# Scores of a pair of chunks as three products of 64 stationary columns on alternating halves of the output

## The chip, the cores and the metric

The kernel runs on one core of a Trainium2 chip. The metric is the device time of one execution in microseconds (us). TensorE multiplies matrices and writes to PSUM, VectorE (DVE) and ScalarE (ACT) work elementwise, GpSimd (POOL) helps them, and SyncE (SP) starts most transfers between HBM and SBUF. Each engine has its own instruction stream and works through it in the order in which the instructions stand; semaphores connect the streams.

## The reference

A block of a streaming encoder on one sequence of 2048 tokens of width 1024. A normalised input is projected (1024 to 2560 columns); one half of the mixer is a gated linear recurrence (HGRN2) of 4 heads of 128 in chunks of 64 tokens, the other a diagonal state-space layer (S5). Their outputs are projected, and a gated MLP with a short convolution follows. What the change touches is the recurrence within a chunk:

```python
b = jnp.cumsum(logf, axis=3)
q_dec = qh * jnp.exp(b)
k_dec = k * jnp.exp(-b)
mask = jnp.tril(jnp.ones((CHUNK, CHUNK), dtype=bool))
att = jnp.einsum('bhnck,bhnsk->bhncs', q_dec, k_dec)
att = jnp.where(mask, att, 0.0)
o_intra = jnp.einsum('bhncs,bhnsv->bhncv', att, vh)
```

A state carries what earlier chunks leave to later ones.

## The kernel before, in words

The program has three stages: projections with recurrence and S5 (its last scores start at 628 us), the output projection (its matmuls from 676 to 892 us), and the MLP. The first stage runs over 80 slots, 40 for each half of the sequence. In a slot `project` (L231 to L233) makes 128 columns of the projection for 512 tokens, 24 matmuls of 128 stationary and 512 moving columns, and hands them to the S5 part or to a unit of the recurrence. A `Unit` is one head and 512 tokens; there are 16 (4 heads, 2 halves, 2 blocks of 512).

A unit joins its 8 chunks of 64 tokens to 4 pairs. It keeps `kt`, for each pair three blocks of 64 key columns: block 0 is the first chunk's keys, block 2 the second's, block 1 the first's keys scaled by the first chunk's whole decay, so that queries of the second chunk can be held against them. `qb` has the queries in the same way; blocks 0 and 2 are the ones read here. `keys` (L628 to L633) and `query` make them on VectorE and ScalarE. `scores` multiplies them into one PSUM tile `pa` of 128 partitions (keys) by 4 pairs of 128 columns (queries): first-chunk keys with first-chunk queries fill partitions 0 to 63 of columns 0 to 63 (L648), and blocks 1 and 2 together, 128 stationary columns, with second-chunk queries fill all partitions of columns 64 to 127 (L649). Keys and queries are float32. VectorE then masks `pa` into `attm`, which a later slot multiplies with the values (`outputs`, L712); `flip_keys` (L667) transposes the scaled keys for the states.

The S5 part has products that the prediction draws on: `scan` (L500) makes 8 matmuls of 64 stationary and 128 moving columns that write partitions 0 to 63 and 64 to 127 by turns; `kernel_rows` (L562 to L565) has small matmuls of 32 stationary columns; `output_map` (L587, L588) has full ones. All are float32.

What order the instructions stand in is set by a scheduler at build time. It takes them as the slots issue them, and places each on its engine by its own estimate of durations, so a change of some instructions can move others by a few places.

Of the kernel before, what the change touches and what calls it, by code (L numbers as in the profile page):

```python
# [41 lines left out]
def _bc(ap, dim, n):  # L42

    a = ap.unsqueeze(dim)
    shape = list(a.shape)
    shape[dim] = n
    return a.to_broadcast(shape)


def _body(ctx, tc, A, out, dbg=None):  # L50
    nc = tc.nc
    VE, SC, GP, PE = nc.vector, nc.scalar, nc.gpsimd, nc.tensor
    dma = nc.sync.dma_start

    def tt(eng, o, a, b, op):
        eng.tensor_tensor(o, a, b, op=op)  # L56
# [91 lines left out]
    with ExitStack() as p1:  # L148
# [451 lines left out]
        class Unit:  # L600
# [43 lines left out]
            def scores(self):  # L644
                pa = ps_od.tile([P, 4, P], F32, tag="od", name="ps_att")
                kt, qb = self.kt, self.qb
                for i in range(4):
                    PE.matmul(pa[0:64, i, 0:64], kt[:, i, 0], qb[:, i, 0], start=True, stop=True)  # L648
                    PE.matmul(pa[:, i, 64:128], kt[:, i, 1:3].rearrange("p b t -> p (b t)"), qb[:, i, 2],  # L649
                              start=True, stop=True)  # L650
                am = attms[self.tb]
                tt(VE, am[0:64, :, 0:64].bitcast(I32), pa[0:64, :, 0:64].bitcast(I32),
                   _bc(mask[0:64, 0:64], 1, 4), ALU.bitwise_and)
                tt(VE, am[:, :, 64:128].bitcast(I32), pa[:, :, 64:128].bitcast(I32),
                   _bc(mask[:, 64:128], 1, 4), ALU.bitwise_and)
                self.ks = hp.tile([P, 4, P], F32, tag="ks", name="ks")
                for i in range(4):
                    SC.activation(self.ks[:, i], kt[:, i, 1:3].rearrange("p b t -> p (b t)"), AF.Copy, scale=self.e2[:, i])
# [100 lines left out]
        for hf in range(2):  # L759
# [12 lines left out]
            for bt in range(8):  # L772
                s0 = 40 * hf + 10 + (27 * bt + 6) // 8
                b = S5(hf, bt)
# [33 lines left out]
        for hf in range(2):  # L808
            for n in range(40):
# [31 lines left out]
                if cb < 4:  # L841
                    if cb % 2 == 0:
                        ut = sp.tile([P, 2, TS, 64], F32, tag="wt", name="ut", bufs=2)
                    t = ut[:, cb % 2]
# [252 lines left out]
    with ExitStack() as p3:  # L1097
        pa = p3.enter_context(ExitStack())
# [530 lines left out]
```

## Time and profile before

| | us |
|---|---|
| median of 3 runs | 2310.33 |
| lowest, highest | 2306.52, 2311.77 |
| profiled execution | 2313.69 |
| its span, first to last instruction | 2311.9 |
| TensorE busy in the span | 2207.9 |
| VectorE busy | 1712.9 |
| ScalarE busy | 990.7 |

The profile's rows name a line of the kernel, an engine, an operation and its tiles as out<-in. PE is TensorE's matmuls, PEld its loads of stationary columns. In a timeline row the first number is the start, the second the time to the end of the last of the instructions that the row merges, xN their count. Ends of matmuls are modelled, so a matmul lasts longer in a row than it holds the array; what counts for pace is the step from start to start. Matmuls in float32 leave two records each; those of the projections, in a rounded float32, leave one.

### The profile page before, as it was taken

How to read it: one execution, taken by the hardware profiler on the slowest of the kernel's cores; microseconds unless marked ns; L12 is line 12 of the kernel's file. 1: busy time of each engine (PE TensorE's matmuls, PEld its weight loads, DVE VectorE, ACT ScalarE, POOL GpSimd, SP SyncE). 2: the span in 40 equal slices, each digit the busy share in tenths (PEclk: the TensorE clock that was granted, in tenths of full speed). 3: DMA queues.
4: the chain of work that ended last, by engine and by line, in shares of the span. 5: the costliest groups of instructions: out<-in, count | busy, mean ns of one | idle time of the engine just before them, and what ended most of it. 6: DMA issues, size and time to landing. Idle time of an engine off the chain costs nothing.

```text
span 2311.9 us, 28187 instructions
## 1 busy us (share of the span) xinstructions
PE 2207.9 (96%) x10120; PEld 1771.8 (77%) x10120; DVE 1712.9 (74%) x2615; ACT 990.7 (43%) x1770; POOL 765.6 (33%) x696
## 2 busy tenths in 40 slices
PE   8999999999989998899999988999999899999996
PEld 6778778888868876688888866888888677777775
DVE  9887786666664325887777778777777688788787
ACT  5333353232254334555555564555555423233343
POOL 1111100000000004555555555655555234445432
PEclk9899999999999999899999988999999999999998
DMA  6465655334434333222222222222222622222223
GB/s 226 143 210 178 188 183 162 124 125 131 141 87 136 116 119 109 83 97 83 83 80 82 78 91 82 93 82 82 83 82 73 227 83 84 71 90 75 68 88 119
DMA packets 143790, 262.18 MB, mean 113 GB/s; under 512 B 43936, under 2 KB 67360, under 8 KB 143648
## 3 DMA queue, kind: packets, MB, share of 16 engines
q1 hardware_dynamic: 138896, 243.05, 32.4%
q0 software_dynamic: 4752, 17.30, 2.0%
q8 instruction: 80, 1.31, 0.2%
q14 instruction: 62, 0.51, 0.1%
HBM read 178.52 MB, written 81.79 MB: 113 GB/s over the span
## 4 chain that ended last, share of the span: by engine, by line
PE 72%; DVE 16%; issue 5%; DMA 3%; ACT 2%; POOL 1%; SPq 0%; DVEq 0%; POOLq 0%; ACTq 0%
PE ps_u L1168 19%; PE ps_v L1168 9%; PE ps_out L975 6%; PE ps_du L1361 6%; PE ps_pj L231 5%; PE ps_pj L233 5%; PE ps_pj L232 5%; PE ps_w L1168 5%; PE ps_dv L1361 3%; DVE accp L62 2%; DVE gvl L65 2%; PE ps_dn L1448 1%; DMA graw<-gv_d 1%; DVE cv L65 1%; PE ps_att L649 1%
## 5 line engine op out<-in xcount | busy, mean ns | idle before, releaser
L231 PE MATMUL ps_pj<-xh,wh 128*128 128x512 f32 x640 | 261.9, 409 | 6.6 <-ACT xh L201 6.4
L232 PE MATMUL ps_pj<-xl,wh 128*128 128x512 f32 x640 | 256.4, 401 | 0.0
L233 PE MATMUL ps_pj<-xh,wl 128*128 128x512 f32 x640 | 256.0, 400 | 0.0
L74 DVE SCALAR_TENSOR_TENSOR cv<-cv,par 128x1024 f32<-128x1024 f32 x176 | 237.1, 1364 | 25.3 <-ACT cv L1180 23.4
L132 ACT ACTIVATE uh<-us 128x512 fp32r<-128x512 f32 x176 | 110.5, 630 | 195.6 <-PE ps_u L1168 93.4
L56 POOL TENSOR_TENSOR us<-uraw 128x512 f32<-128x512 f32 x88 | 121.8, 1384 | 215.4 <-DMA uraw<-in_wup_dram 149.7
L65 DVE TENSOR_TENSOR ul<-us,uh 128x512 fp32r<-128x512 f32 x132 | 156.2, 1184 | 1.6 <-ACT uh L132 1.5
L1361 PE MATMUL ps_du<-dh,gvh 128*128 128x512 f32 x320 | 131.9, 412 | 25.3 <-DVE accp L62 16.8
L132 ACT ACTIVATE uh<-uraw 128x512 fp32r<-128x512 f32 x132 | 83.5, 632 | 159.0 <-PE ps_u L1168 81.0
L231 PEld LDWEIGHTS ps_pj<-xh,wh 128*128 128x128 f32 x640 | 121.9, 190 | 37.2 <-ACT xh L201 6.4
L233 PEld LDWEIGHTS ps_pj<-xh,wl 128*128 128x128 f32 x640 | 121.6, 190 | 29.5 <-issue 1.1
L232 PEld LDWEIGHTS ps_pj<-xl,wh 128*128 128x128 f32 x640 | 121.7, 190 | 28.2 <-issue 1.5
L1361 PE MATMUL ps_du<-dl,gvh 128*128 128x512 f32 x320 | 128.6, 402 | 0.0
L1361 PE MATMUL ps_du<-dh,gvl 128*128 128x512 f32 x320 | 128.6, 402 | 0.0
L65 POOL TENSOR_TENSOR ul<-us,uh 128x512 fp32r<-128x512 f32 x44 | 68.6, 1560 | 173.0 <-ACT uh L132 170.6
L132 ACT ACTIVATE gvh<-gs 128x512 fp32r<-128x512 f32 x80 | 50.4, 630 | 162.3 <-POOL gs L56 81.6
L62 DVE TENSOR_TENSOR accp<-accp,ps_du 128x1024 f32<-128x1024 f32 (+1 forms) x84 | 97.7, 1163 | 28.7 <-PE ps_du L1361 28.3
L1180 ACT ACTIVATE cv<-cv,par 128x1024 f32<-128x1024 f32 x88 | 109.7, 1246 | 19.3 <-DVE cv L62 17.9
L56 POOL TENSOR_TENSOR gs<-graw 128x512 f32<-128x512 f32 x38 | 58.6, 1542 | 160.8 <-DMA graw<-gv_d 135.0
L1361 PEld LDWEIGHTS ps_du<-dh,gvh 128*128 128x128 f32 x320 | 61.7, 193 | 48.9 <-issue 23.8
L975 PE MATMUL ps_out<-wo,ogp 128*128 128x512 f32 x384 | 95.5, 404 | 0.9 <-DVE og L74 0.9
L515 POOL MEMSET z<- 128x4 f32 x16 | 1.7, 104 | 284.7 <-DVE zi L65 212.7
(438 smaller groups left out, 6237.4 us busy)
## 6 DMA issues: line engine op xcount, KB each, us to landing
uraw<-in_wup_dram SPq DMA_DIRECT2D x86, 512.0 KB, 3.5
gv_d<-cv SPq DMA_DIRECT2D x43, 512.0 KB, 2.6
graw<-gv_d SPq DMA_DIRECT2D x84, 256.0 KB, 3.3
wraw<-in_win_dram SPq DMA_DIRECT2D x24, 512.0 KB, 4.5
xt<-in_wdown_dram SPq DMA_DIRECT2D x44, 256.0 KB, 3.0
ws_d<-wh POOLq DMA_DIRECT2D x16, 512.0 KB, 3.5
ws_d<-wl POOLq DMA_DIRECT2D x16, 512.0 KB, 6.0
wh<-ws_d SPq DMA_DIRECT2D x16, 512.0 KB, 4.0
```

Source lines behind the costliest of these rows:

```text
L56: eng.tensor_tensor(o, a, b, op=op)
L62: eng.tensor_tensor(o, a, b, op=ALU.add)
L65: eng.tensor_tensor(o, a, b, op=ALU.subtract)
L74: eng.scalar_tensor_tensor(o, a, s, b, op0=op0, op1=op1)
L132: SC.activation(h, raw, AF.Copy)
L231: PE.matmul(ps, a, xh, start=(kt == 0), stop=False)
L232: PE.matmul(ps, a, xl, start=False, stop=False)
L233: PE.matmul(ps, b, xh, start=False, stop=(kt == KT - 1))
L975: PE.matmul(pss[nh], parts[lp][kt][:, tq], wo[rp][kt][:, nh * BLK : (nh + 1) * BLK], start=first, stop=last)
L1168: PE.matmul(ps, l, r[kt], start=(fresh and first), stop=end, skip_group_check=not fresh)
L1180: SC.activation(c, cin[:, 2 : HALF + 2], AF.Identity, scale=tap[2], bias=par[:, C_CB + cb : C_CB + cb + 1])
L1361: PE.matmul(ps[:, i], l[:, j, i * P : (i + 1) * P], r, start=(fresh and n == 0), stop=(n == 5), skip_group_check=not fresh)
```

## The change

The two products of a pair become three. All have 64 stationary and 64 moving columns. The product of 128 stationary columns is cut into its halves: block 2 with the second chunk's queries goes to partitions 64 to 127, block 1 with the same queries to partitions 0 to 63. The first product stays. In the order of issue a pair writes partitions 0 to 63, 64 to 127, 0 to 63. A unit has 12 matmuls instead of 8, and TensorE 64 more in all.

```diff
                 for i in range(4):
-                    PE.matmul(pa[0:64, i, 0:64], kt[:, i, 0], qb[:, i, 0], start=True, stop=True)
-                    PE.matmul(pa[:, i, 64:128], kt[:, i, 1:3].rearrange("p b t -> p (b t)"), qb[:, i, 2],
-                              start=True, stop=True)
+                    for rows, cols, k, q in ((0, 0, 0, 0), (64, 64, 2, 2), (0, 64, 1, 2)):
+                        PE.matmul(pa[rows : rows + 64, i, cols : cols + 64], kt[:, i, k], qb[:, i, q],
+                                  start=True, stop=True)
```

In the scheduled order fifteen of the sixteen units now stand as twelve matmuls in a row on TensorE. The fifth unit (237 us in the trace of before) is the other one. There products of the S5 output map, `ps_y`, stand between the scores `ps_att`:

```order
-L648 MATMUL ps_att<-qb,kt 64x64
+L649 MATMUL ps_att<-qb,kt 64x64 x2
 L587 MATMUL ps_y<-ug,mt 128x128
-L649 MATMUL ps_att<-qb,kt 128x64
-L648 MATMUL ps_att<-qb,kt 64x64
+L649 MATMUL ps_att<-qb,kt 64x64 x10
 L588 MATMUL ps_y<-xs,tv 128x128
-L649 MATMUL ps_att<-qb,kt 128x64
-L648 MATMUL ps_att<-qb,kt 64x64
-L649 MATMUL ps_att<-qb,kt 128x64
-L648 MATMUL ps_att<-qb,kt 64x64
-L649 MATMUL ps_att<-qb,kt 128x64
```

Before, two of these products stood between scores; now one does, and the other stands behind all twelve.

Other rows move by a few places. One such place on TensorE is behind the seventh unit (312 us), where the S5 scan's products, `ps_b`, stand among the projections, `ps_pj`:

```order
 L231 MATMUL ps_pj<-xh_156,wh 128x512
 L232 MATMUL ps_pj<-xl_158,wh 128x512
+L500 MATMUL ps_b<-ug,tw 64x128 x8
 L233 MATMUL ps_pj<-xh_156,wl 128x512
-L500 MATMUL ps_b<-ug,tw 64x128 x8
 L231 MATMUL ps_pj<-xh_156,wh 128x512
 L232 MATMUL ps_pj<-xl_158,wh 128x512
```

The eight products of the scan moved ahead of one projection matmul.

## Rows read from the trace of the kernel before

**Rows 1.** Page, busy us by engine; sum of the stretches from 160 to 640 us.
```profile
PE 2207.9 (96%) x10120; PEld 1771.8 (77%) x10120; DVE 1712.9 (74%) x2615; ACT 990.7 (43%) x1770; POOL 765.6 (33%) x696
...
sum 480.00, PE 477.88 PEld 389.70 DVE 337.89 ACT 177.51 POOL 18.93; mean PE 79.65 PEld 64.95 DVE 56.32 ACT 29.58 POOL 3.16
```

**Rows 2.** Waits of TensorE up to 700 us: total, times, longest (us).
```profile
PE ps_ot L728 <- DVE on L59: 6.4, 1, 6.4
PE ps_k L564 <- DVE v L65: 5.1, 1, 5.1
...
PE ps_att L648 <- DVE kt L59: 0.8, 1, 0.8
...
PE ps_b L500 <- DMA ug<-u_d: 0.5, 1, 0.5
PE ps_k L565 <- DVE v L74: 0.3, 1, 0.3
```

**Rows 3.** Timeline of the second unit, matmuls (PE) and weight loads (PEld).
```profile
106.15 0.33 PE L648 MATMUL ps_att<-qb,kt 128*64 128x64 f32 x2
106.40 0.43 PE L649 MATMUL ps_att<-qb,kt 128*128 128x64 f32 x2
106.77 0.33 PE L648 MATMUL ps_att<-qb,kt 128*64 128x64 f32 x2
...
106.14 0.19 PEld L648 LDWEIGHTS ps_att<-qb,kt 128*64 128x64 f32 x2 [0.37 <-issue]
...
108.49 0.19 PEld L232 LDWEIGHTS ps_pj<-xl,wh 128*128 128x128 f32 x1
```

**Rows 4.** Timeline of an S5 scan behind transposes; the scan's records, ns min/median/max.
```profile
124.57 0.60 PE L667 MATMUL ps_vn<-ident,vt 128*128 128x128 f32 x4
125.10 1.09 PE L500 MATMUL ps_b<-ug,tw 128*64 128x128 f32 x16
...
125.10 0.85 PEld L500 LDWEIGHTS ps_b<-ug,tw 128*64 128x64 f32 x16 [0.17 <-issue]
126.12 0.19 PEld L231 LDWEIGHTS ps_pj<-xh,wh 128*128 128x128 f32 x1 [0.17 <-issue]
...
L500 PE MATMUL ps_b<-ug,tw x256: 272/273/324, 76.7 to 612.0; 128*64 128x128 f32 x128
```

**Rows 5.** Timeline of small S5 products of 16 moving columns.
```profile
142.63 0.23 PE L562 MATMUL ps_k<-sbc,bd 128*32 128x16 f32 x2
142.71 0.21 PE L563 MATMUL ps_k<-nci,bd 128*32 128x16 f32 x2
```

**Rows 6.** First unit's ends; projections in its stretch; stretches (PE first, clock third last).
```profile
92.66 0.29 PEld L648 LDWEIGHTS ps_att<-qb,kt 128*64 128x64 f32 x2 [0.36 <-issue]
...
96.53 0.33 PEld L233 LDWEIGHTS ps_pj<-xh,wl 128*128 128x128 f32 x1
...
100.15 0.63 PE L232 MATMUL ps_pj<-xl,wh 128*128 128x512 f32 x1
100.58 0.50 PE L233 MATMUL ps_pj<-xh,wl 128*128 128x512 f32 x1
...
87.00:101.00 14.00, 13.25 (x45) 9.62 (x46) 12.39 (x24) 5.69 (x18) 1.40 (x6) 0.51 0.43 115
...
551.30:554.80 3.50, 3.50 (x18) 3.38 (x18) 3.50 (x6) 0.61 (x3) 0.00 (x0) 0.51 0.90 303
```

**Rows 7.** Timeline, the last projections of the stage.
```profile
649.38 0.40 PE L232 MATMUL ps_pj<-xl,wh 128*128 128x512 f32 x1
649.61 0.40 PE L233 MATMUL ps_pj<-xh,wl 128*128 128x512 f32 x1
```

**Rows 8.** Busy time 220 to 240 us (VectorE third); VectorE's way to the fifth unit's keys.
```profile
220.00:240.00 20.00, 19.24 (x100) 15.54 (x99) 19.88 (x47) 6.66 (x17) 1.79 (x5) 1.00 0.40 145
...
214.87 0.69 DVE L59 TENSOR_TENSOR f<-ps_pj,rx 128x512 f32<-128x512 f32 x1 [4.26 <-PE ps_pj L233]
...
236.83 0.68 DVE L59 TENSOR_TENSOR kt<-k,rec 128x512 f32<-128x512 f32 x1
```

## The prediction

> **What bounds the kernel now.** I read the page first, for the engine that is busiest: TensorE, busy for 2207.9 of 2311.9 us [rows 1]. An average over stages doesn't say what the stage of the change is worth, so next came the table by stretch: the scores lie between 92 and 629 us, and from 160 to 640 us TensorE is busy for 477.9 of 480 us, VectorE for 337.9 [rows 1]. A busy engine may still be one that waits inside its instructions, so third came the list of who waited for whom: up to 700 us TensorE's waits are a handful, and those of over 2 us lie before the first scores and behind the last; in between the longest is 0.8 us [rows 2]. So time taken from TensorE here should come off the end, as long as VectorE, which feeds it, keeps up. The stages behind are chained to this one, with no work that has a date of its own.
>
> **What a unit of scores costs now.** Sixteen units (4 heads, 2 halves, 2 blocks) make 4 pairs of chunks each. A float32 matmul stands in the trace as two records (x2), each with its own weight load. In the second unit the first weight load of the scores starts at 106.14, that of the projection behind them at 108.49, so 2.35 us for 8 matmuls [rows 3]. Starts go in a fixed step: 0.25 us from the matmul of 64 columns to that of 128, 0.37 back, 0.62 per pair. That is long: a float32 record of 128 stationary columns and 128 moving ones takes 0.11 us in the transposes, (0.60-0.27)/3 for four of them, with 0.27 for a record's own length, taken from the scan's, which has as many moving columns [rows 4]. And here there are four records per pair with half the moving columns, which would be at most 0.44. The rest arises where the width changes between 64 and 128 columns, 8 times in a unit (once into it and 7 times inside).
>
> **What takes their place.** Twelve matmuls of 64 columns by 64, all of one width, on halves 0, 1, 0 of the output partitions. The trace has a group of just this kind: the S5 scan's input products, 8 matmuls of 64 columns that alternate between the halves, with 128 moving columns. Its 16 records start 0.055 us apart, (1.09-0.27)/15 [rows 4]. Each half then gets a record every 0.109 us, the step of a record of 128 moving columns that has the array for itself, so the halves work side by side. The whole group takes 1.02 us from its first weight load (125.10) to that of the projection behind it (126.12): 8 records of one half, 0.875, and 0.147 for the first load and the way back to 128 columns.
>
> In the new scores half 0 has 8 matmuls, 16 records, each with half as many moving columns. By proportion (an estimate from [rows 4]) a record takes 0.0547 us, so half 0 needs 16 x 0.0547 = 0.875, as in the scan, and half 1, with 4 matmuls, lies beside it. A unit then costs 1.02 us instead of 2.35: 1.33 saved. The bounds: if a record of 64 moving columns takes as long as one of 128, half 0 needs 16 x 0.109 + 0.147 = 1.89, saving 0.46; if both halves of the traffic could be spread evenly, 12 x 0.0547 + 0.147 = 0.80, saving 1.55. I take 1.33, since the scan's group is the nearest row in width, order of halves and place. Weight loads of 64 columns need no more time than the records: in the scan they ran ahead of them (16 loads within 0.85) [rows 4].
>
> Could the number of instructions itself be the price, 24 records instead of 16? Records of 16 moving columns start within 0.04 us of each other, two from 142.63 to 142.71 [rows 5], under the 0.055. [...]
>
> **The sum.** Fourteen units like the second: 14 x 1.33 = 18.6. The fifth has two products of S5 between its scores now; in the new order one still splits it in 2 and 10, which costs one more change of width each way, 0.15 by the scan's overhead: 1.2. [...] Twice 1.02 would save 1.83. If the clock still rises at 101 us, that time is filled with projections that start 0.43 apart instead of 0.23 [rows 6, 7], worth 1.83 x 0.23/0.43 = 1.0, the value I take (the other end is 1.8). Together 20.8 us.
>
> What could take some back: from 100 to 320 us VectorE is full at times, 19.88 of 20 us from 220 on [rows 8], and TensorE has three waits there of 0.3 to 0.8 us [rows 2]. A faster TensorE meets each of them earlier, by at most one unit's 1.33 where scores lie between the start of VectorE's work and the wait: 3 x 1.33 = 4.0 at most, nothing at least. The biggest burst starts with a projection (214.87) and ends with the keys for the fifth unit (236.83) [rows 8]; no scores lie between, so that wait moves along unchanged. I take 1.0. In return VectorE has the scores to mask earlier. The moves of the scheduler elsewhere are by a few rows on TensorE and VectorE (a transposition of keys five projections later, S5 products past one projection), all in the first half of the stage; I cost them at nothing because TensorE has other work queued on both sides, and their cover gone would be a wait of the size in [rows 2], 0.3 to 0.8 each.
>
> So 19.8 us. The profiled execution took 2313.7 us (span 2311.9 and 1.8 around it), which gives 2293.9; the median of the runs is 3.4 lower, so I forecast 2310.3 - 19.8 = 2290.5 us. [...]
>
> **Rivals, with chances.** Forecast, halves side by side and little given back: 0.62, time 2290.5.
>
> (a) The halves take turns, since 64 moving columns are over before the other half's matmul arrives, or since two matmuls in a row on half 0 hold up the queue. Then 24 x 0.0547 + 0.147 = 1.46 per unit, saving 0.89; over 15.6 units' worth, less 1.0, 12.9 us: 2297. For it: in the scan the halves strictly alternate, here half 0 comes twice in a row. Against: there too each matmul's two records stand in a row on one half. 0.13.
>
> (b) VectorE becomes the bound from 100 to 320 us, and all that units 2 to 8 save there is given back, 6 x 1.33 + 1.2 = 9.2: 2310.3 - 20.8 + 9.2 = 2299. For it the full stretch; against, VectorE is idle for 142 of 480 us from 160 to 640 [rows 1], while the units there bring TensorE forward by under 20. 0.11.
>
> (c) A record doesn't get shorter with fewer moving columns: 0.46 x 15.6 = 7.2 us, 2303. Against it the records of 16 columns. 0.06.
>
> [...] Chance 0.04.
>
> (e) The change does what it says (twelve matmuls of 64 columns stand in the new order), but moved rows bring new waits that eat it: 2310. It would take waits of 20 us in a stage that has under 3 in its middle. 0.04.
>
> **How the numbers follow.** A measurement here tells 0.2%, 4.6 us, from no change. Forecast and (a) to (c) are faster by more, 0.92; (e) the same, 0.04; (d) slower, 0.04. Forecast's own spread is 2285 to 2296 (saving per unit up to 1.55, given back up to 4, the clock's 1.7, the spread of runs). To leave out no more than 2 in 10 the range takes in (a), (b) and (c) at its edge: 2284 to 2303.
>
> **What would show it.** In the changed profile: a plain unit's first load to the next projection's at about 1.02 us (1.46 for (a), 1.9 for (c), over 2.35 for (d)); starts of its records under 0.04 us apart on the mean, in pairs on the two halves; TensorE's busy time down by about 20 us with its waits from 100 to 320 us up by no more than 1 or 2; the end of the last projection of the stage, now 650.0 us [rows 7], at about 630. The prediction is wrong if the units are as short as this and the end moves by under 10 us, or if a plain unit stays above 1.5 us.

## The result, and the profile after

The change is faster. Its executions have a median of 2288.58 us (2287.12 to 2293.58) against 2310.2 for the kernel before; the ratio is 0.9911, with a 95% interval of 0.9898 to 0.9925. A second comparison on another occasion gave 2287.16 us and 0.9916 (0.9902 to 0.9929). The forecast was 2290.5 us, a gain of 19.8; measured were 21.6 and 19.0 between the medians.

The page of the changed kernel, and the sum of busy times by stretch from 160 to 640 us, as in [rows 1]:

```profile
PE 2183.3 (95%) x10248; PEld 1753.7 (77%) x10248; DVE 1717.5 (75%) x2615; ACT 993.0 (43%) x1770; POOL 776.8 (34%) x696
...
sum 480.00, PE 476.22 PEld 390.30 DVE 347.92 ACT 188.22 POOL 18.76; mean PE 79.37 PEld 65.05 DVE 57.99 ACT 31.37 POOL 3.13
```

TensorE has 128 records more and is busy for 24.6 us less than in the first trace of the kernel before (2207.9; two further traces of that kernel have 2201.7 and 2200.2, so some of the difference is the execution's). It is still what bounds the stage, 476.2 of 480 us. The profiled execution (2293.58 us) is the slowest of its four.

The second unit of the changed kernel, matmuls and then weight loads, answers to [rows 3]:

```profile
104.36 1.15 PE L649 MATMUL ps_att<-qb,kt 128*64 128x64 f32 x24
105.44 0.50 PE L232 MATMUL ps_pj<-xl,wh 128*128 128x512 f32 x1
...
104.36 1.01 PEld L649 LDWEIGHTS ps_att<-qb,kt 128*64 128x64 f32 x24 [0.37 <-DVE attm L56]
105.44 0.19 PEld L232 LDWEIGHTS ps_pj<-xl,wh 128*128 128x128 f32 x1
```

From the first load of the scores to that of the next projection it is 1.08 us instead of 2.35. The 24 records start 0.04 us apart on the mean, (1.15-0.22)/23, where 0.22 is a record's own length:

```profile
L649 PE MATMUL ps_att<-qb,kt x384: 222/222/271, 95.6 to 607.8; 128*64 128x64 f32 x192
...
  DVE attm L56: 2.7, 3
```

The second of these rows says that VectorE's masking now waits 2.7 us in all for the scores; in the kernel before it was 15.1:

```profile
  DVE attm L56: 15.1, 7
```
The end of the stage, [rows 7], has moved from 649.61 to 629.06:

```profile
629.06 0.40 PE L233 MATMUL ps_pj<-xh,wl 128*128 128x512 f32 x1
```

Waits of TensorE from the first scores to 320 us, the changed kernel; they answer to the last rows of [rows 2]:

```profile
PE ps_k L565 <- DVE v L74: 1.2, 2, 1.0
PE ps_kst L667 <- ACT vn L673: 0.9, 1, 0.9
PE ps_att L649 <- DVE kt L59: 0.8, 1, 0.8
PE ps_b L500 <- DMA ug<-u_d: 0.3, 1, 0.3
```

Together 3.2 us, where the kernel before had 0.8 + 0.5 + 0.3 = 1.6. One wait is new, that of the transposed keys `ps_kst` for ScalarE's values `vn`, and one has grown.

### The profile page after: what moved, and what is told of

Its sections match the earlier page's. It is cut to its first block, busy times and chain, and to the rows that moved or that the text cites. A ratio compares the mean times of both kernels' runs of the same rounds, so it can differ in the third digit from the quotient of the medians.

```text
span 2291.6 us, 28447 instructions
## 1 busy us (share of the span) xinstructions
PE 2183.3 (95%) x10248; PEld 1753.7 (77%) x10248; DVE 1717.5 (75%) x2615; ACT 993.0 (43%) x1770; POOL 776.8 (34%) x696
## 4 chain that ended last, share of the span: by engine, by line
PE 69%; DVE 19%; DMA 4%; issue 4%; ACT 2%; POOL 1%; SPq 0%; DVEq 0%; POOLq 0%; ACTq 0%
PE ps_u L1168 19%; PE ps_v L1168 9%; PE ps_out L975 8%; PE ps_du L1361 5%; PE ps_w L1168 5%; PE ps_pj L231 4%; PE ps_pj L233 4%; PE ps_pj L232 4%; PE ps_dv L1361 2%; DVE accp L62 2%; DMA graw<-gv_d 2%; DVE gvl L65 2%; PE ps_dn L1448 2%; DVE cv L65 1%; DVE dl L65 1%
## 5 line engine op out<-in xcount | busy, mean ns | idle before, releaser
L1180 ACT ACTIVATE cv<-cv,par 128x1024 f32<-128x1024 f32 x88 | 109.9, 1249 | 19.1 <-DVE cv L62 17.8
L975 PE MATMUL ps_out<-wo,zp 128*128 128x512 f32 x384 | 94.7, 402 | 0.0
```

Source lines behind the costliest of these rows:

```text
L975: PE.matmul(pss[nh], parts[lp][kt][:, tq], wo[rp][kt][:, nh * BLK : (nh + 1) * BLK], start=first, stop=last)
L1180: SC.activation(c, cin[:, 2 : HALF + 2], AF.Identity, scale=tap[2], bias=par[:, C_CB + cb : C_CB + cb + 1])
```

## The experiments

**Where the gain comes from.** Two things differ inside a unit: it no longer changes between 64 and 128 stationary columns (its width), and the halves can work side by side. Four variants take them apart. In the diffs, minus is the change and plus the variant, unless said otherwise.

*The products of before, sorted by width* (plus against the kernel before):

```diff
                 for i in range(4):
                     PE.matmul(pa[0:64, i, 0:64], kt[:, i, 0], qb[:, i, 0], start=True, stop=True)
+                for i in range(4):
                     PE.matmul(pa[:, i, 64:128], kt[:, i, 1:3].rearrange("p b t -> p (b t)"), qb[:, i, 2],
```

> The two products of before, but all four of 64 columns first and then all four of 128, so a unit changes width twice instead of 8 times, and no halves work side by side. Theory (both the missing width changes and the halves side by side make the gain): 8 records x 0.058 + 0.055, one change of 0.1, 8 weight loads of 128 columns x 0.107: about 1.5 us per unit instead of 2.35, so some 13 us gained, 2297 us. Rival A (only the halves side by side matter, a change of width costs nothing): 2.35 per unit still, 2310. Rival B (only the width changes matter): nearly the whole gain, about 1.1 per unit, 2290.

Weight loads of its eighth unit:

```profile
314.10 0.54 PEld L648 LDWEIGHTS ps_att<-qb,kt 128*64 128x64 f32 x8 [0.37 <-issue]
314.71 0.97 PEld L650 LDWEIGHTS ps_att<-qb,kt 128*128 128x128 f32 x8
315.59 0.19 PEld L231 LDWEIGHTS ps_pj<-xh,wh 128*128 128x128 f32 x1
```

1.49 us per unit, as the theory had it. Rival A is out, since the instructions are those of before, and B too, since it is not 1.1. Six changes of width less save 0.86 us, 0.14 each. Measured: 2290.95 us, 0.9925 of before (0.9913 to 0.9938), better than the 2297 expected. Against the 2308.46 of the kernel before on this occasion that is 17.5 us, some 4 more than the 13 expected; on these 4 see the first unit, in the part on the prediction.

*All twelve on one half:*

```diff
-                    for rows, cols, k, q in ((0, 0, 0, 0), (64, 64, 2, 2), (0, 64, 1, 2)):
+                    for rows, cols, k, q in ((0, 0, 0, 0), (0, 64, 2, 2), (0, 64, 1, 2)):
```

> Twelve matmuls of 64 columns as in the change, but all of them write partitions 0 to 63 (the second chunk's own scores are overwritten there and left out of the mask). No change of width within a unit, no work side by side. Theory: 24 records x 0.058 + 0.15 = 1.55 us per unit instead of 1.07, 16 x 0.47 = 7.5 us slower than the change, 2296. Rival B (the halves take turns anyway, all the gain is from the width): 1.07 per unit, 2288.6 as the change. Rival A (all the gain is from the halves): back to 2.35 per unit, 2310.

```profile
316.58 1.47 PEld L649 LDWEIGHTS ps_att<-qb,kt 128*64 128x64 f32 x24 [0.37 <-DVE rs_t L74]
318.12 0.19 PEld L231 LDWEIGHTS ps_pj<-xh,wh 128*128 128x128 f32 x1
```

1.54 us for the same 24 records that take 1.08 in the change: without the second half they stand in a line, 0.058 apart, (1.47-0.14)/23 with 0.14 for a load's own length. So the halves side by side are worth 0.46 us a unit, on top of the width. Without them the cut of the wide product gains nothing, 1.54 against the 1.49 of the sorted variant: there the eight records of 128 stationary columns start 0.111 us apart, (0.97-0.19)/7 with 0.19 for a load's own length, as far as records with twice the moving columns [rows 4], and each is now two records of 0.058. The whole took 2290.11 us, 0.9917 (0.9904 to 0.993), some 6 us better than the 2296 expected. The units don't explain that; whole times a few us apart don't separate these variants from each other, the units and the stage (below) do.

*Without the product on the second half:*

```diff
-                    for rows, cols, k, q in ((0, 0, 0, 0), (64, 64, 2, 2), (0, 64, 1, 2)):
+                    for rows, cols, k, q in ((0, 0, 0, 0), (0, 64, 1, 2)):
```

> The change without its product on partitions 64 to 127 (the second chunk's own scores are left out): 8 matmuls of 64 columns on one half. Theory: that half sets the time and the other rode along for nothing, so 16 records x 0.058 + 0.15 = 1.08 us per unit, 2288.6 as the change. Rival (the halves share something, by time or by number of records): 8 of 12 matmuls, about 0.75 us per unit, 5 us faster, 2283.5.

```profile
312.11 1.01 PEld L649 LDWEIGHTS ps_att<-qb,kt 128*64 128x64 f32 x16 [0.37 <-issue]
313.19 0.19 PEld L231 LDWEIGHTS ps_pj<-xh,wh 128*128 128x128 f32 x1
```

1.08 us, the time of the change to the hundredth: the four matmuls on the second half cost TensorE nothing. The whole is at 2285.13 us, 0.9898 (0.9885 to 0.9911), less than the 2288.6 expected and more than the rival's 2283.5, but the units leave the rival no room. Part of it is shorter waits of TensorE, 1.4 us in all from the first scores to 320 us where the change has 3.2 and, in a second trace, 2.9. The 16 records stand 0.058 apart here too, (1.01-0.14)/15, though no two products write the same place, as two of three do in the variant on one half.

*Another order, half 0 twice and then half 1:*

```diff
-                    for rows, cols, k, q in ((0, 0, 0, 0), (64, 64, 2, 2), (0, 64, 1, 2)):
+                    for rows, cols, k, q in ((0, 0, 0, 0), (0, 64, 1, 2), (64, 64, 2, 2)):
```

> The change with its three products in another order: partitions 0 to 63 twice, then 64 to 127. Theory (half 0 sets the time, half 1 lies beside it in any order): 1.07 us per unit, at most one matmul of half 1 left over at the end, 0.06 to 0.12 more; time as the change within 2 us. Rival (the alternation is what brings the gain): the halves overlap less, 1.3 to 1.55 us per unit, 4 to 8 us slower than the change.

```profile
315.36 1.01 PEld L649 LDWEIGHTS ps_att<-qb,kt 128*64 128x64 f32 x24 [0.37 <-DVE rs_t L74]
316.43 0.19 PEld L231 LDWEIGHTS ps_pj<-xh,wh 128*128 128x128 f32 x1
```

1.07 us for its eighth unit, and 2285.87 us, 0.9911 (0.9898 to 0.9925), where the change ran on the same chip with 0.9916. That the halves alternate from one matmul to the next isn't needed. How far apart in the order their work may stand, no run shows.

**Can it go further?** *Two products per pair*, the first with 128 moving columns:

```diff
-                    for rows, cols, k, q in ((0, 0, 0, 0), (64, 64, 2, 2), (0, 64, 1, 2)):
-                        PE.matmul(pa[rows : rows + 64, i, cols : cols + 64], kt[:, i, k], qb[:, i, q],
-                                  start=True, stop=True)
+                    PE.matmul(pa[0:64, i], kt[:, i, 0], qb[:, i, 0:2].rearrange("p b t -> p (b t)"), start=True, stop=True)
+                    PE.matmul(pa[64:128, i, 64:128], kt[:, i, 2], qb[:, i, 2], start=True, stop=True)
```

Block 1 of the queries carries the decay that block 1 of the keys carried.

> Two products per pair, both of 64 columns: block 0 of the keys with blocks 0 and 1 of the queries, 128 moving columns, on partitions 0 to 63, and block 2 with block 2 on 64 to 127. Same moving columns per half as in the change, but 16 records instead of 24. Theory: half 0 needs 8 records x 0.109 + 0.147 = 1.02 us per unit, 0.05 less than the change, 0.8 us in all, 2287.8 and not to be told from 2288.6. Rival (the number of records sets the price): two thirds, about 0.75 us per unit, 5 us faster, 2283.5.

Its eighth unit, first load and the next projection's:

```profile
315.58 0.13 PEld L648 LDWEIGHTS ps_att<-qb,kt 128*64 128x64 f32 x1 [0.37 <-ACT qb L642]
...
316.60 0.19 PEld L233 LDWEIGHTS ps_pj<-xh,wl 128*128 128x128 f32 x1 [0.17 <-issue]
```

1.02, as expected, and so in twelve of the fifteen units that no other product splits; the other three take 1.06 to 1.08. The moving columns of the fuller half count, the records hardly (16 take 1.02 us, 24 take 1.08). Measured 2286.05 us, 0.9903 (0.989 to 0.9916), not to be told from the change. Its waits are longer, one of 3.0 us for ScalarE's `vn`.

*The halves balanced*, on top of that (minus is the variant before). In every second pair the chunks change places; the lines on masks and values are left out here:

```diff
-                    PE.matmul(pa[0:64, i], kt[:, i, 0], qb[:, i, 0:2].rearrange("p b t -> p (b t)"), start=True, stop=True)
-                    PE.matmul(pa[64:128, i, 64:128], kt[:, i, 2], qb[:, i, 2], start=True, stop=True)
+                    lo, hi = (slice(0, 64), slice(64, 128))[:: -1 if i % 2 else 1]
+                    PE.matmul(pa[lo, i], kt[:, i, 0], qb[:, i, 0:2].rearrange("p b t -> p (b t)"), start=True, stop=True)
+                    PE.matmul(pa[hi, i, 64:128], kt[:, i, 2], qb[:, i, 2], start=True, stop=True)
...
+                for i in range(1, 4, 2):
+                    for b in range(2):
+                        SC.activation(self.ks[:, i, 64 - 64 * b : 128 - 64 * b], kt[:, i, 1 + b], AF.Copy, scale=self.e2[:, i])
```

> The two products per pair of the variant before, but in every second pair the chunks change places on the partitions (keys, values, masks and scales with them; three more small operations on VectorE and four on ScalarE per unit). Each half then streams 2 x 128 + 2 x 64 columns of a unit instead of 4 x 128 and 4 x 64. Theory (the fuller half sets the time, as if alone): 4 records x 0.109 + 4 x 0.0547 + 0.147 = 0.80 us per unit instead of 1.02, 16 x 0.22 = 3.5 us less, 0.9895 of the kernel before. Rival (VectorE and ScalarE, which do more, give it back): units of 0.80, but longer waits of TensorE between 100 and 320 us, no faster than the variant with 1.02.

```profile
300.79 0.13 PEld L651 LDWEIGHTS ps_att<-qb,kt 128*64 128x64 f32 x1 [0.37 <-ACT qb L644]
...
301.62 0.19 PEld L233 LDWEIGHTS ps_pj<-xh,wh 128*128 128x128 f32 x1
```

0.83 us for this unit, its seventh, 0.80 expected. But only nine units are like it (0.82 to 0.84). Two take 1.06 and 1.08, and the other five are split by products that the scheduler put between the scores, as the eighth by a projection, which costs width changes again:

```profile
311.06 0.13 PEld L651 LDWEIGHTS ps_att<-qb,kt 128*64 128x64 f32 x1 [0.36 <-ACT qb L644]
...
311.55 0.19 PEld L234 LDWEIGHTS ps_pj<-xl,wh 128*128 128x128 f32 x1
311.98 0.13 PEld L651 LDWEIGHTS ps_att<-qb,kt 128*64 128x64 f32 x1 [0.24 <-issue]
...
312.46 0.19 PEld L235 LDWEIGHTS ps_pj<-xh,wl 128*128 128x128 f32 x1
```

1.40 us, of which a projection of 0.23 is not the unit's own: nothing gained over 1.08. So the 16 x 0.22 of the expectation didn't come; nine units give 9 x 0.25 = 2.2. TensorE's waits from the first scores to 320 us are 2.1 us; behind that one of 1.3 for ScalarE's queries stands where the change has 0.7. So VectorE and ScalarE hide most of their additions. It has the lowest median of the study, 2283.27 us and 0.9889 of before (0.9873 to 0.9905). Against the change, 0.9911 and 0.9916, that would be 5 to 6 us, but the intervals overlap and the two didn't run side by side, so a gain over the change in the whole time is not shown.

*The stage by itself.* The whole times hold the later stages too, and these differ by execution: from the last unit's scores to the end it is 1684.8 and 1679.6 us in two traces of the change, 1680.5 to 1685.8 in three of the kernel before. From the first unit's first load to the last unit's, one number for each trace (the first includes the low clock at 551 us [rows 6]):

| | us |
|---|---|
| before | 533.5, 531.8, 531.7 |
| sorted by width | 515.6 |
| all on one half | 517.3 |
| the change | 511.2, 511.5 |
| another order | 511.5 |
| two products | 511.3 |
| without the second half | 509.6 |
| halves balanced | 508.1 |

Here the variants stand as their units and waits have them, and the balanced one is some 3 us ahead of the change, in its one trace.

**The first unit and the clock.** In the kernel before, the first unit ran at a granted clock of 0.51 and the clock fell again at 551 us [rows 6]; in the changed kernel's first trace it took 1.07 us at a granted clock of 1.00 (94.5 to 98 us), and the clock stays at 1.00 from 100 to 640. Whether that belongs to the change was open. The kernel before got two more traces without an edit, and the change a second one.

> The kernel before, unchanged, for a second trace. [...] Theory C (the old scores, with their gaps, keep or bring the low clock): the first unit takes about 3.9 us again, or low stretches stand beside units of scores between 100 and 640 us. Rival (chance of the execution): the first unit takes 2.35 us and there is no low stretch up to 640 us, as in the others.

> The kernel before once more, a third trace, with the same two readings: under theory C the first unit takes about 3.9 us or a low stretch stands beside scores between 100 and 640 us; under the rival neither, in at least one of the two traces.

> The changed kernel again, on one chip with the variant below and with more executions. Units at 1.07 us again (theory). The wait of 1.6 us at 72 us and those of 1.0 us at 140 and 194 us: if the moved rows bring them they are there again, if they are the execution's they are not. Time 0.990 to 0.992 of the kernel before, 2288 us. No low clock between 95 and 640 us under theory C; under its rival such a stretch may stand here as well as in the kernel before.

The first load of the first unit, and the stretch from 96 to 98 us with the granted clock third from the end, in the third trace of the kernel before:

```profile
93.66 0.29 PEld L648 LDWEIGHTS ps_att<-qb,kt 128*64 128x64 f32 x2 [0.36 <-issue]
...
96.00:98.00 2.00, 2.00 (x9) 1.65 (x8) 2.00 (x6) 0.68 (x3) 0.00 (x0) 0.50 1.03 271
```

and in the second trace of the change:

```profile
93.15 1.58 PEld L649 LDWEIGHTS ps_att<-qb,kt 128*64 128x64 f32 x24 [0.36 <-issue]
...
91.00:94.50 3.50, 3.50 (x33) 2.36 (x32) 1.89 (x3) 1.75 (x6) 1.30 (x5) 0.51 0.33 75
...
96.00:98.00 2.00, 2.00 (x10) 1.59 (x10) 2.00 (x5) 1.07 (x4) 0.00 (x0) 1.00 1.02 280
```

All three traces of the kernel before have the first unit at 3.87 us (granted clock 0.50) and 13.7 us of low clock. In both traces of the change the clock had risen by 94.5 us (1.00 from there to 96); in the second, scores had begun 1.3 us earlier at the low one. The low stretch at 551 us [rows 6] is in neither new trace of the kernel before (clock 1.00 from 550 to 556 in the third, and stages of 531.8 and 531.7 us where the first trace has 533.5): an accident of one execution. Of the waits, the one of 1.6 us at 72 us was the execution's, those for `v` and `vn` of 1.0 us each came again, and no trace of the kernel before has one for them above 0.4, so they come with the change; whether by the moved rows or by the faster units is not separated.

*The change with its first unit in the form of before* should tell whether the old scores hold the clock down (theory C: 3.87 us for that unit again, and 13.7 us of low clock):

```diff
+                if self.first and self.h == 0:
+                    for i in range(4):
+                        PE.matmul(pa[0:64, i, 0:64], kt[:, i, 0], qb[:, i, 0], start=True, stop=True)
+                        PE.matmul(pa[:, i, 64:128], kt[:, i, 1:3].rearrange("p b t -> p (b t)"), qb[:, i, 2],
+                                  start=True, stop=True)
+                else:
...
```

> The change with the first unit alone in the form of before (8 matmuls, two widths). [...] Rival (the clock rose late by chance in three traces of before): 2.35 us for the unit at full clock, 1.3 us slower, not to be told from the change.

> The change with the first unit alone in the form of before, a second trace. In its first trace the clock had risen at 94.0 us, before that unit (95.3), which took 2.35 us. In three traces of the kernel before the unit took 3.87 us and the clock rose only 4.3 us behind its end, in eight traces with another first unit it rose by 95.6 us. Theory C in a weaker form (the old first unit holds the low clock if the clock hasn't risen before it, which differs by execution): 3.87 us and 13.7 us of low clock in at least one of the two further traces. Rival (something else of the kernel before keeps the clock low): 2.35 us in both.

> The same once more, a third trace, with the same two readings: 3.87 us for the first unit and 13.7 us of low clock in at least one of the two under the weaker theory C, 2.35 us in both under its rival.

First trace of this kernel:

```profile
95.30 0.19 PEld L649 LDWEIGHTS ps_att<-qb,kt 128*64 128x64 f32 x2 [0.38 <-issue]
...
91.00:94.50 3.50, 3.50 (x14) 2.36 (x14) 3.29 (x5) 2.41 (x6) 0.00 (x0) 0.57 0.30 67
94.50:96.00 1.50, 1.50 (x11) 0.84 (x9) 0.19 (x2) 0.59 (x3) 0.81 (x5) 1.00 0.13 29
```

In all three of its traces the clock had risen before the unit began (at 94.0, 94.4 and 92.9 us, scores at 95.3, 94.9 and 94.6), and the unit took 2.35 us. Its time, 2288.69 us and 0.9919 (0.9905 to 0.9933), can't be told from the change. So theory C in its strong form falls, and the weak form got no trace in which it could have shown itself: none of the three began the old unit at the low clock. What stands is a count. Where the old scores began at the low clock (three traces), it stayed low until 3.9 to 4.3 us behind their end; where the new ones or their variants did (the change's second trace, the variant on one half, the other order, the balanced one), it rose 0.1 to 1.3 us after their start. The old unit isn't what puts the clock down, since it fell at 87 to 89 us, ahead of the first scores, and whether it or the moment of the rise in each execution keeps it there is not settled.

## Why the prediction was right, and which term was off

**What bounds the stage** was read rightly: time taken from TensorE between 92 and 629 us came off the end, and little of it was given back later. In the third trace of before against the change's second, the first scores start at 93.66 and 93.15, the last unit's at 625.31 and 604.60:

```profile
625.31 0.19 PEld L648 LDWEIGHTS ps_att<-qb,kt 128*64 128x64 f32 x2 [0.37 <-issue]
...
604.60 1.01 PEld L649 LDWEIGHTS ps_att<-qb,kt 128*64 128x64 f32 x24 [0.37 <-DVE xc L62]
```

From first to last that makes 20.2 us, and the last unit's own 1.27 comes on top, 21.5 in all; the spans are 2305.8 and 2284.2, 21.6 apart.

**The unit** was forecast at 1.02 us by proportion from the S5 scan, and is 1.08. The step of a record on the fuller half is 0.058 us instead of 0.0547, 16 records in a line, as the variant with one half shows. Saved are 1.27 and not 1.33 per plain unit: 17.8 for the fourteen instead of 18.6. The fifth unit gives 0.96 instead of 1.2, taking its scores' start to the next projection: 241.30 - 237.56 before, 236.62 - 233.84 now.

**Side by side**, the point on which rival (a) hung, is shown by two variants: 1.54 without it, and no price for the second half's four matmuls. (a) would have made 1.46. Rivals (c), 1.9 us, and (d), a slower unit of over 2.35, fall with the unit's time of 1.08. The number of records isn't the price either: it is 1.08 us with 24 of them and with the 16 that are left without the second half.

**VectorE as the next bound**, rival (b), didn't come. The waits in its stretch grew by 1.3 us (2.9 against 1.6, second trace of the change and third of before), where 1.0 was taken. With that (e) is out as well.

**The term that was off** is the first unit. The prediction let the clock rise at 101 us all the same and took 1.0 us, with 1.8 as the other end. Between the third trace of before and the second of the change it is 2.2 us for the unit (3.87 and 1.64) and 1.8 for the projections behind it, from the unit's end to the second unit 9.42 and 7.66 us, because they ran at a granted clock of 0.50 from 97.5 to 101.4 before (0.43 apart and not 0.23, as in [rows 6, 7]): 4.0 us. What was wrong in it is the assumption that the clock rises when it did before. Whether it is the change that makes it rise earlier is not shown (above); at a granted clock of 1.00 in both kernels the unit would give 1.27 (2.35 - 1.08), by estimate, and the sum below 18.8. The same term explains the sorted variant: its first unit began with the clock up and took 1.49 instead of 3.87, which with the projections is some 3 of the 4 us that its units don't give. It doesn't explain the variant on one half, whose expectation was worked out from the change and so has this gain in it; in the stage that variant is 5.8 to 6.1 us behind the change, near what its units ask for (15 x 0.46 = 6.9 up to the last). Two of the forecast's numbers on the clock were the author's estimates. Its 1.83 is 3.87, the first unit at the low clock [rows 6], less twice 1.02: no run shows a whole unit of the new scores at the low clock, only the 1.64 us with the rise inside, and the old unit takes 3.87 us at 0.50 and 2.35 at 1.00, 1.65 times. The clock's 1.7 in its spread is for a stretch like the 3.5 us at 0.51 from 551 us on [rows 6]: the first trace of before, which has it, is longer in the stage by 1.7 and 1.8 us than the other two.

By terms, for these two traces: 17.8 + 1.0 + 4.0 - 1.3 = 21.5 us, as the stage shows. The forecast had 18.6 + 1.2 + 1.0 - 1.0 = 19.8. Its nearness to the 19.0 and 21.6 of the medians owes something to luck, errors of opposite sign: 3.0 us too little for the first unit, 1.3 too much for the others and the waits.

## What to carry to other kernels

When small float32 matmuls of different widths alternate, count the changes of width before the columns: sorting them by width, with no other edit, took these units from 2.35 to 1.49 us. A product of 128 stationary columns whose neighbour has 64 can be cheaper as two of 64 on the two halves (1.08 us a unit here, and 1.54 with all on one half); here the half with more moving columns then set the time (1.08 us with the other half's products and without), so balance the halves (0.82 to 0.84 us in nine units) and not the number of instructions, and look whether other products still stand between them. A group in the same kernel that already has the shape wanted, here the scan, is a good price list: 1.02 us by it, 1.08 measured.

## What was not expected of the hardware

A record of 64 columns by 64 steps at 0.058 us in a line, a little over half of the 0.109 of 128 moving columns [rows 4]; with 128 stationary columns the same halving of the moving columns gains nothing, 0.111. And the clock at the start of the scores differs between kernels by more than their work: low for 13.7 us in three of three traces before, for 3.4 to 6.8 us in eleven of eleven with other scores (three of them with the first unit as before), which is worth 1.8 to 1.9 us in the projections and, for the old first unit, 1.5 (3.87 instead of 2.35). The cause is open.
